# Moving the start of h, of the constant matrices and of the weight slots in SBUF: a decoder trunk on one Trainium2 core

## The chip, the core and the metric

The kernel runs on one core of a Trainium2 chip. The metric is the device time of one launch in microseconds (us). The core has a matrix engine (PE in the views; its weight loads are listed apart as PEld), a vector engine (DVE), a scalar engine (ACT), a small general engine (POOL) and a queue that only issues DMAs (SP). The operands of all of them lie in SBUF, which has 128 partitions; a tile takes the same bytes of every partition, and "address" below means the byte within a partition at which a tile begins. Matrix products go to PSUM.

## What is computed

A residual stream of 512 tokens by 1024 channels goes through two layers. Each layer has a SwiGLU block, a mixer and a second SwiGLU block, each between two RMS norms:

```python
def _swiglu(h, w_gate, w_up, w_down):
    return (jax.nn.silu(h @ w_gate) * (h @ w_up)) @ w_down

for l in range(DEPTH):                      # DEPTH = 2
    g = norm_g[l]
    f = _swiglu(_rmsnorm(x, g[0]), ffn_w_gate[l, 0], ffn_w_up[l, 0], ffn_w_down[l, 0])
    x = x + 0.5 * _rmsnorm(f, g[1])
    m = _mixer(_rmsnorm(x, g[2]), w_in[l], conv_w[l], pool_w[l], pool_scale[l], w_out[l])
    x = x + _rmsnorm(m, g[3])
    f = _swiglu(_rmsnorm(x, g[4]), ffn_w_gate[l, 1], ffn_w_up[l, 1], ffn_w_down[l, 1])
    x = x + 0.5 * _rmsnorm(f, g[5])
```

The hidden width of SwiGLU is 2816. The mixer projects `h @ w_in`, feeds the pieces to 8 heads of a stick-breaking attention, a short convolution and a pooling, and multiplies the result by `w_out`. All data are float32.

## The kernel before

**Three products for one.** Every large float32 product is made of three matmuls of a reduced float32 type: each operand is split into a high part and a low part, and the products high x high, high x low and low x high are summed in PSUM (`mm3`, L271 to L274, and `token_mms`, L384 to L393). One `mm(dst, w, r, ...)` at L222 issues each of them: `w` is the stationary operand (a load of 128 columns), `r` the moving one (up to 512 columns). Nearly all matmuls carry the line L223, so they are told apart by tile names.

**The normalised input.** `hHs` and `hLs` (L187, L188; `hh` and `hl` in the views) hold the high and low part of the normalised, transposed input h of the block at hand, 8 x 512 values to a partition each. They are allocated once and rewritten at each norm by `prenorm` (L315).

**Slots.** Everything else of size lives in 28 slots of 4 KB to a partition (`slot`, L124): raw weights as they arrive (`raw`), their high and low parts (`wh`, `wl`, made by ACT at L155 and DVE at L156), the hidden activations (`hid`), the mixer's outputs (`mix`), attention's operands (`q`, `qk`, `v`), partial sums (`f`) and gains (`g`). Smaller temporaries come from a third pool (`t`, `c`, `ss`, `pH`, `pL`).

**Which product takes what.**
- Gate and up of a SwiGLU block, and the mixer's projections (`unit`, L276): stationary a weight slot, moving h. In the views `psz<-hh,wh`, `psz<-hl,wh`, `psz<-hh,wl` (psd for the projections).
- The mixer's values (`values`, L602): stationary h, moving a weight slot: `psz<-wh,hh`, `psz<-wl,hh`, `psz<-wh,hl`.
- Down (`stream`, L395, and `by_tokens`, L421): stationary `hid`, moving a weight slot. No h in it: `psz<-wh,hid`, `psz<-wl,hid`.
- The output projection (`by_halves`, L407, and `by_tokens`): stationary `mix`, moving a weight slot. No h in it.
- Values and down have the same pattern: one block of 128 tokens of the stationary tile, then 512 columns of the moving one, three such matmuls for each pair of blocks.

**Widths.** A SwiGLU block works through its 22 blocks of hidden width in chunks of 8, 8 and 6. In the first chunk three blocks (HEAD, L32) run over half the tokens at a time, with 256 moving columns; all others have 512.

**Order.** The PE's order is written out by `line` and `after` (L214 to L220): each matmul is made to follow the one issued before it. Attention runs as a side task that is polled between matmuls, due at times counted in estimated matmul durations. Weights are loaded and split ahead as slots come free (`ahead`, L162).

**Addresses.** A pool hands out tiles in the order of the requests and rounds each tile's size up to a multiple of 32 bytes. `cpool` comes first: cst (L184), x, mat, hh, hl, ntri, none_, identr, maskr, expo (L196). Behind it follow `wpool` with the 28 slots and `apool` with the temporaries. `cst` is 50 floats (200 bytes, rounded to 224), `expo` one float (4 bytes, rounded to 32); all the others are multiples of 512 bytes.

Of the kernel before, what the change touches and what calls it, by code (L numbers as in the profile page):

```python
# [8 lines left out]
F32 = mybir.dt.float32  # L9
# [6 lines left out]
P = 128  # L16
# [42 lines left out]
C_END = C_PSC + DEPTH * 2  # L59
# [42 lines left out]
def trunk_kernel(ctx: ExitStack, tc: tile.TileContext, xt: bass.AP, wu: bass.AP,  # L102
                 consts: bass.AP, mats: bass.AP, gains: bass.AP, out: bass.AP):
    nc = tc.nc
    cpool = ctx.enter_context(tc.tile_pool(name="cpool", bufs=1))
# [75 lines left out]
        give(2 * n)  # L181


    cst = cpool.tile([P, C_END], F32, name="cst")  # L184
    x = cpool.tile([P, TBS, D], F32, name="x")
    mat = cpool.tile([P, M_END], F32, name="mat")
    hHs = cpool.tile([P, KB, T], F32R, name="hh")  # L187
# [5 lines left out]
    none_ = cpool.tile([P, P], F32R, name="none_")  # L193
    identr = cpool.tile([P, P], F32R, name="identr")
    maskr = cpool.tile([P, P], F32R, name="maskr")
    expo = cpool.tile([P, 1], F32, name="expo")  # L196
    nc.vector.memset(expo, -0.5)

    def tmp(shape=(P, T), dt=F32, tag="t", bufs=TB):
# [709 lines left out]
```

## Time and profile before

| | us |
|---|---|
| median of 3 runs | 1954.72 (1954.02 to 1956.04) |
| profiled execution, device time | 1954.8 |
| its span, first to last instruction | 1953.0 |
| PE busy | 1914.8 (98%) |
| DVE busy | 856.9 (44%) |
| ACT busy | 714.0 (37%) |

The PE has 9072 matmuls and 9072 weight loads. Its busy time is the union of the listed durations; matmuls overlap (a listed one of 512 columns lasts about 400 ns, and the next begins some 230 ns later). What a matmul costs in a stretch without waits is therefore read from the distance between starts: the length of the stretch over the count of matmuls in it. The chain of waits gives just that, since it runs from each matmul's start to the next one's.

### The profile page before, as it was taken

Reading aid. Unit: us, or ns where it says so; the run is one execution under the profiler, and the core shown is the slowest. Engines: PE = TensorE matmul, PEld = TensorE weight load, DVE = VectorE, ACT = ScalarE, POOL = GpSimd, SP = SyncE. Lnnn points to the kernel's source line nnn. Section 1 sums busy time; section 2 is a strip of 40 time slices with the busy share of each in tenths; the row PEclk is TensorE's granted clock in tenths of the full one; section 3 lists DMA queues with packets and bytes.
Section 4 is the critical chain, followed back from the end, with each engine's and each line's share of the span. In section 5 each row is a group of like instructions: output and inputs, shape, how many; then the busy total and the mean of one; then the engine's idle time right before and its main releaser. Section 6 shows DMA issues by size and latency. Waiting matters only on the chain.

```text
span 1953.0 us, 21947 instructions
## 1 busy us (share of the span) xinstructions
PE 1914.8 (98%) x9072; PEld 1588.2 (81%) x9072; DVE 856.9 (44%) x1090; ACT 714.0 (37%) x1089; POOL 40.9 (2%) x68
## 2 busy tenths in 40 slices
PE   8999999999999999999999999999999999999998
PEld 6888888878878888888898888887888888888886
DVE  4423342557766323333463232336577563223333
ACT  4323222346764323222342322224477542222221
POOL 0000000000001000000000000000000000000000
PEclk8999999999999999999999999999999999999999
DMA  5322232131122223233142322322111232322311
GB/s 211 101 83 101 85 137 79 59 116 43 44 97 109 97 68 127 76 110 106 43 152 87 109 74 80 136 81 103 66 49 44 81 141 86 106 79 85 130 65 44
DMA packets 50645, 180.17 MB, mean 92 GB/s; under 512 B 5744, under 2 KB 5872, under 8 KB 50544
## 3 DMA queue, kind: packets, MB, share of 16 engines
q1 hardware_dynamic: 50544, 178.76, 26.3%
q8 instruction: 71, 1.16, 0.2%
q14 instruction: 30, 0.25, 0.0%
HBM read 176.65 MB, written 2.10 MB: 92 GB/s over the span
## 4 chain that ended last, share of the span: by engine, by line
PE 92%; DVE 4%; ACT 2%; DMA 1%; issue 1%; POOL 0%; SPq 0%; POOLq 0%; DVEq 0%; ACTq 0%
PE psz L223 80%; PE psd L223 11%; DMA raw<-in_w_dram 1%; DVE wl L156 1%; PE psd L265 1%; ACT t L296 0%; DVE hl L331 0%; DVE pL L509 0%; DVE f L321 0%; ACT t L538 0%; ACT pH L508 0%; POOL ss L312 0%; DVE t L541 0%; DVE x L375 0%; DVE f L357 0%
## 5 line engine op out<-in xcount | busy, mean ns | idle before, releaser
L223 PE MATMUL psz<-hl,wh 128*128 128x512 f32 (+1 forms) x1536 | 574.8, 374 | 7.2 <-DVE hl L331 6.2
L223 PE MATMUL psz<-hh,wh 128*128 128x512 f32 (+1 forms) x1536 | 575.0, 374 | 1.3 <-ACT hh L330 1.3
L223 PE MATMUL psz<-hh,wl 128*128 128x512 f32 (+1 forms) x1536 | 573.9, 374 | 0.0
L156 DVE TENSOR_TENSOR wl<-raw,wh 128x1024 fp32r<-128x1024 f32 x324 | 386.5, 1209 | 322.6 <-ACT wh L155 249.9
L223 PE MATMUL psz<-wh,hid 128*128 128x512 f32 x1408 | 437.3, 390 | 0.0
L155 ACT CAST wh<-raw 128x1024 fp32r<-128x1024 f32 x324 | 328.9, 1038 | 233.9 <-PE psz L223 177.5
L223 PEld LDWEIGHTS psz<-hl,wh 128*128 128x128 f32 x1536 | 292.2, 190 | 63.3 <-DVE hl L331 7.0
L223 PEld LDWEIGHTS psz<-hh,wh 128*128 128x128 f32 x1536 | 292.0, 190 | 57.4 <-ACT hh L330 2.4
L223 PEld LDWEIGHTS psz<-hh,wl 128*128 128x128 f32 x1536 | 292.1, 190 | 55.2
L223 PEld LDWEIGHTS psz<-wh,hid 128*128 128x128 f32 x1408 | 264.3, 188 | 55.0
L223 PE MATMUL psz<-wl,hid 128*128 128x512 f32 x704 | 274.0, 389 | 0.0
L444 DVE TENSOR_TENSOR t<-t,psz 128x512 f32<-128x512 f32 x84 | 57.7, 686 | 489.0 <-PE psz L223 489.0
L445 ACT CAST hid<-t 128x512 fp32r<-128x512 f32 x88 | 54.7, 622 | 462.4 <-DVE t L444 462.4
L296 ACT ACTIVATE t<-psz 128x512 f32<-128x512 f32 (+1 forms) x136 | 77.4, 572 | 238.3 <-PE psz L223 237.5
L223 PEld LDWEIGHTS psz<-wl,hid 128*128 128x128 f32 x704 | 132.2, 188 | 27.4
L223 PE MATMUL psd<-hh,wh 128*128 128x512 f32 (+1 forms) x320 | 121.0, 378 | 0.0
L223 PE MATMUL psd<-hl,wh 128*128 128x512 f32 (+1 forms) x320 | 119.2, 373 | 0.0
L223 PE MATMUL psd<-hh,wl 128*128 128x512 f32 (+1 forms) x320 | 119.2, 373 | 0.0
L446 DVE TENSOR_TENSOR hid<-t,hid 128x512 fp32r<-128x512 f32 x88 | 60.9, 692 | 60.9 <-ACT hid L445 60.9
L223 PEld LDWEIGHTS psd<-hh,wl 128*128 128x128 f32 x320 | 60.2, 188 | 11.6
L223 PEld LDWEIGHTS psd<-hh,wh 128*128 128x128 f32 x320 | 60.2, 188 | 11.2 <-PE psd L223 0.5
L223 PEld LDWEIGHTS psd<-hl,wh 128*128 128x128 f32 x320 | 60.2, 188 | 11.2 <-issue 0.5
(99 smaller groups left out, 1377.3 us busy)
## 6 DMA issues: line engine op xcount, KB each, us to landing
raw<-in_w_dram SPq DMA_DIRECT2D x316, 512.0 KB, 3.3
g<-in_gains_dram SPq DMA_DIRECT2D x12, 512.0 KB, 5.2
x<-in_xt_dram SPq DMA_DIRECT2D x4, 512.0 KB, 8.5
raw<-in_w_dram SPq DMA_DIRECT2D x8, 256.0 KB, 2.7
out_dram<-x SPq DMA_DIRECT2D x8, 256.0 KB, 2.1
mat<-in_mats_dram SPq DMA_DIRECT2D x1, 384.0 KB, 9.4
mat<-in_mats_dram SPq DMA_DIRECT2D x1, 64.0 KB, 3.2
cst<-in_consts_dram SPq DMA_DIRECT2D x1, 25.0 KB, 9.1
```

The costliest lines, as they stand in the source:

```text
L155: nc.scalar.copy(h[:, :n], raw[:, :n])
L156: nc.vector.tensor_tensor(lo[:, :n], raw[:, :n], f32(h[:, :n]), op=ALU.subtract)
L223: ins = nc.tensor.matmul(dst, w, r, start=start, stop=stop, skip_group_check=True)
L265: ins = nc.tensor.transpose(dst, src, ident)
L296: ins = nc.scalar.activation(out_, in_, f_, **kw)
L444: nc.vector.tensor_tensor(u, g, pu, op=ALU.mult)
L445: nc.scalar.copy(t[:, 0, :], u)
L446: nc.vector.tensor_tensor(t[:, 1, :], u, f32(t[:, 0, :]), op=ALU.subtract)
```

## The change

```diff
-    cst = cpool.tile([P, C_END], F32, name="cst")
+    cst = cpool.tile([P, 64], F32, name="cst")[:, :C_END]
     x = cpool.tile([P, TBS, D], F32, name="x")
     mat = cpool.tile([P, M_END], F32, name="mat")
     hHs = cpool.tile([P, KB, T], F32R, name="hh")
...
-    expo = cpool.tile([P, 1], F32, name="expo")
+    expo = cpool.tile([P, 64], F32, name="expo")[:, 0:1]
     nc.vector.memset(expo, -0.5)
```

`cst` and `expo` are each allocated with 64 floats (256 bytes); the part in use is the same as before. What stands behind them moves. In the built programs the tiles begin here:

| tile | before | modulo 64, 256, 512 | after | modulo 64, 256, 512 |
|---|---|---|---|---|
| cst | 16512 | 0, 128, 128 | 16512 | 0, 128, 128 |
| x | 16736 | 32, 96, 352 | 16768 | 0, 128, 384 |
| mat | 33120 | 32, 96, 352 | 33152 | 0, 128, 384 |
| hh | 36704 | 32, 96, 352 | 36736 | 0, 128, 384 |
| hl | 53088 | 32, 96, 352 | 53120 | 0, 128, 384 |
| ntri, none_, identr, maskr (first) | 69472 | 32, 96, 352 | 69504 | 0, 128, 384 |
| expo | 71520 | 32, 96, 352 | 71552 | 0, 128, 384 |
| slots (first of 28) | 71552 | 0, 128, 384 | 71808 | 0, 128, 128 |
| t (first) | 186240 | 0, 128, 384 | 186496 | 0, 128, 128 |
| pH, pL (first) | 200832 | 0, 128, 128 | 201088 | 0, 128, 384 |

Slices that a matmul reads begin at multiples of 512 bytes within their tile, so the columns hold for them too. No instruction is added, removed or moved: on each of the five engines' queues the instructions, their waits and the tiles that they name stand in the same order as before, row by row; only the line numbers behind the edit are one higher.

## Rows read from the trace of the kernel before

**Rows 1.** The page: engines' busy time, then the chain's shares by line.

```profile
PE 1914.8 (98%) x9072; PEld 1588.2 (81%) x9072; DVE 856.9 (44%) x1090; ACT 714.0 (37%) x1089; POOL 40.9 (2%) x68
...
PE psz L223 80%; PE psd L223 11%; DMA raw<-in_w_dram 1%; DVE wl L156 1%; PE psd L265 1%; ACT t L296 0%; DVE hl L331 0%; DVE pL L509 0%; DVE f L321 0%; ACT t L538 0%; ACT pH L508 0%; POOL ss L312 0%; DVE t L541 0%; DVE x L375 0%; DVE f L357 0%
```

**Rows 2.** Whole chain, its long pieces: start us, length us, engine, output, matmul count.

```profile
41.08 14.20 PE psz L223 x120
58.12 322.35 PE psz L223 x1395
...
408.94 9.10 PE psz L223 x39
418.04 14.70 PE psd L223 x63
...
1540.62 20.41 PE psz L223 x90
...
1612.41 332.54 PE psz L223 x1440
```

**Rows 3.** Chain within 158:246, a stretch of gate and up; same columns.

```profile
157.89 88.20 PE psz L223 x378
```

**Rows 4.** Chain within 248:290, the stretch of down that follows.

```profile
247.95 42.17 PE psz L223 x186
```

**Rows 5.** Chain within 1022:1077, gate and up of a later block.

```profile
1022.09 55.06 PE psz L223 x236
```

**Rows 6.** Chain within 1078:1121, down of that block.

```profile
1077.85 43.31 PE psz L223 x191
```

**Rows 7.** PE groups by tiles and shape: count, busy us, mean ns, idle before.

```profile
L223 PE MATMUL psz<-hl,wh 128*128 128x512 f32 x1216 | 481.1, 396 | 0.0
...
L223 PE MATMUL psd<-hl,wh 128*128 128x512 f32 x256 | 101.2, 395 | 0.0
...
L223 PE MATMUL psz<-hh,wl 128*128 128x256 f32 x320 | 92.9, 290 | 0.0
...
L223 PE MATMUL psz<-wl,hh 128*128 128x512 f32 x64 | 25.3, 395 | 0.0
...
L223 PE MATMUL psd<-hh,wl 128*128 128x256 f32 x64 | 18.0, 281 | 0.0
```

**Rows 8.** Window of the first block: PE, PEld, DVE, ACT, POOL; clock, DMA, GB/s.

```profile
58.00:380.40 322.40, 322.40 (x1398) 262.04 (x1397) 107.95 (x115) 87.99 (x114) 1.65 (x3) 1.00 0.26 89
```

**Rows 9.** Who the PE waited for, attention: total us, times, longest.

```profile
PE psz L223 <- DVE pL L509: 5.6, 10, 1.0
...
PE psz L223 <- ACT pH L508: 3.4, 2, 2.1
```

**Rows 10.** PE timeline, attention's values, behind the output projection: start us, length.

```profile
553.16 0.39 PE L223 MATMUL psz<-pH,v 128*128 128x512 f32 x1
553.39 0.39 PE L223 MATMUL psz<-pL,v 128*128 128x512 f32 x1
553.61 0.33 PE L223 MATMUL psz<-pH,v 128*128 128x384 f32 x1
...
553.96 0.28 PE L223 MATMUL psz<-pH,v 128*128 128x256 f32 x1
554.08 0.29 PE L223 MATMUL psz<-pL,v 128*128 128x256 f32 x1
554.20 0.23 PE L223 MATMUL psz<-pH,v 128*128 128x128 f32 x1
```

**Rows 11.** PE timeline, attention's values again, behind a projection that moves h.

```profile
450.38 0.39 PE L223 MATMUL psz<-pH,v 128*128 128x512 f32 x1
450.61 0.40 PE L223 MATMUL psz<-pL,v 128*128 128x512 f32 x1
450.85 0.33 PE L223 MATMUL psz<-pH,v 128*128 128x384 f32 x1
```

## The prediction, made before the changed kernel ran

> **What bounds the kernel now.** I read the page first. PE is busy 1914.8 us of the 1953.0 us span, and the chain that ends last runs on the matmul line for 80% (psz) and 11% (psd) [rows 1]: the time is a sum of matmuls, so whatever changes the cost of one matmul shows, and hardly anything else does. Next the long pieces of the chain. The first SwiGLU block, from the end of its narrow matmuls on, is one piece of 322.35 us with 1395 matmuls and no other engine in it, and the last block one of 332.54 us with 1440 [rows 2]. In the window of the first one DVE works 107.95 us of 322.40, ACT 87.99, the DMA engines 0.26 of their time, at a granted clock of 1.00, that is 2.4 GHz [rows 8]. So in these stretches nothing feeds the PE late and the clock does not change. What is left is the matmul's own cost, and there the reader is to see that it has two values:
>
> - Gate and up: 88.20 us for 378 matmuls, 233.3 ns each [rows 3]; in a later block 55.06 us for 236, 233.3 ns [rows 5].
> - Down: 42.17 us for 186, 226.7 ns [rows 4]; in the later block 43.31 us for 191, 226.8 ns [rows 6].
>
> All have 512 moving columns, the same types and the same three-product pattern, one weight load for each matmul. The block's chain checks it: of the 1395 matmuls 912 are gate and up (38 units of 24), 483 down; 912 x 0.2333 + 483 x 0.2267 = 322.3 us, the piece's length. In the last block 912 and 528 make 332.5 us [rows 2].
>
> Which operand makes 233 of 227? The other stretches tell. The projections (moving h) take 14.70 us for 63, 233.3 ns; the mixer's values (stationary h, moving a weight slot) take 9.10 us for 39, 233.3 ns; the output projection (no h) takes 20.41 us for 90, 226.8 ns [rows 2]. Values and down differ in one thing only: the stationary tile is h in one and a slot in the other. So a matmul that reads h, on either side, costs 6.6 ns more, 2.9%. In the table of addresses h begins at 32 modulo 64, every slot at 0. The trace cannot prove that the address is the reason, but h's address is what the edit changes.
>
> **The change part by part.**
>
> Padding cst costs 56 bytes of SBUF and moves x, mat, h and the four 128x128 constants by 32 bytes. Padding expo keeps the slots at 0 modulo 64: h and slots then have the same start modulo 256, as `hid` and the weight slots of down have had all along. No instruction is added or moved, so no queue is passed and no wait arises; the DMAs, their sizes and order stay. The sum therefore has one kind of term: matmuls that read h, times 6.6 ns, as far as they lie on the chain.
>
> Gate and up with 512 columns: three groups of 1216 (one is shown) [rows 7], 3648 matmuls x 6.6 ns = 24.1 us. All lie in pieces where the chain is PE alone [rows 2], with the other engines at a third of the time [rows 8]; a PE that is 2 to 3% faster stays the bound. All of it counts.
>
> Values: three groups of 64 [rows 7], 192 x 6.6 = 1.3 us. Their longest stretch is PE alone too [rows 2]; it counts.
>
> Projections with 512 columns: three groups of 256 [rows 7], 768 x 6.6 = 5.1 us. They share the mixer with attention's chain through ACT and DVE, which does not get faster, and the PE already waits there, 5.6 us for pL and 3.4 us for pH [rows 9]. Since the PE's order is fixed, what the projections save ahead of such a wait is given back in it. Bounds: 0 and 5.1 us. I take half, 2.5 us, because most of the projections' matmuls stand ahead of such a wait or behind it with nothing to tell which.
>
> Gate, up and projections with 256 columns: three groups of 320 and three of 64 [rows 7], 1152 matmuls, now 14.20 us for 120, 118.3 ns [rows 2]. If the cost goes by columns, they fall to half of 226.7, 113.4 ns: 5.7 us gained. If what is over is fixed per matmul, they come to what attention's 256-column products with all operands at 0 modulo 64 take: 553.96 to 554.20 is 0.24 us for two, 120 ns [rows 10], 1.9 us lost. That row is the nearest, and with its steps of 10 ns it cannot be told from 118.3. I take 0 and keep both ends.
>
> Attention's constants (ntri, none_, identr as stationary, 336 short matmuls): at most 336 x 6.6 ns = 2.2 us, at least nothing; they stand beside waits, I take 0. The transposes with mat as an operand, and ACT's and DVE's work on x and h: no row shows these at another address. Three per cent either way of the transposes is under 1 us, and the engines are two thirds idle; 0.
>
> Here a rule speaks against the change. Every row above with h is dearer than every row without it [rows 3 to 6]. The Trainium skill, page "TensorE: Matmul & The Clock Gate", section "Back-to-back issue gap", gives N/2.4 + 2.5 ns between warm matmuls whatever they read, 215.8 ns for 512 columns (an estimate from that page). By it the start of a tile has no part in the time and the sum would be nothing. This trace has 226.7 and 233.3 ns at the full clock, so it does not agree; still, what it would make of the time is the first rival below.
>
> Sum: 24.1 + 1.3 + 2.5 + 0 = 27.9 us, against the profiled execution's 1954.8 us, which stands at the median of 1954.72: **1926.9 us**. The ends: 24.1 + 1.3 + 5.1 + 5.7 + 2.2 + under 1 = 39, 1916 us; 24.1 + 1.3 + 0 - 1.9 - under 1 = 23, 1932 us.
>
> **The rivals.**
>
> *The dearer matmul is h's, but not by its start.* The tiles hh and hl differ from slots in more: they are read by some 2900 matmuls of each layer, are written in four pieces by token block, and lie elsewhere in SBUF. If that is the reason, or if 32 modulo 64 is as good as 0, every matmul keeps its cost: 1954.8 us. For it: nothing in this trace has a slot at 32 modulo 64 or h at 0. Against it: the surcharge is the same to 0.1 ns with h stationary or moving, in SwiGLU blocks and mixers, and the address is what all of these share. The Trainium skill bears on it: "SBUF — State Buffer", Door 1, speaks of 16-byte lines, of which 32 modulo 64 is a whole number, and "Who interferes with whom" says that PE's two reads do not wait on anyone; by that the times would stay. No run here shows lines, and the two costs show that some operands do cost more.
>
> *A new distance.* After the change h begins at 384 modulo 512 and the slots at 128, 256 bytes apart; in down stationary and moving are 0 apart modulo 512. The trace has one pair that is 256 apart with both at 0 modulo 64: attention's values, pH and pL against v. Behind the output projection two of them take 553.16 to 553.61, 225 ns each [rows 10]; behind a projection 450.38 to 450.85, 235 ns each [rows 11]. If 235 is what that distance costs, the 4608 wide matmuls with h go from 233.3 to 235: +1.7 ns x 4608 = 7.8 us slower, 1962.6 us. It decides from 234.2 ns on (0.2% of the time over 4608 matmuls is 0.85 ns). Against it is rows 10, at the same distance; rows 11 may be what the h matmuls ahead of it leave behind.
>
> *Part of it.* One of the two reads stays dear, or attention's waits grow by more than the projections save: the gain is 4 to 20 us, 1935 to 1951 us.
>
> That the change does not do what it says is out: the addresses of the built program are those of the table.
>
> **How the numbers follow.** A measurement of this kernel can tell about 0.2%, 4 us, from no change. Forecast, 1916 to 1935 us: 0.80. More than that: 0.02. Part of it: 0.04. No change: 0.09. New distance, slower: 0.05. The predicted time is the forecast's, 1926.9 us. The range 1916 to 1935 takes in the ends of the sum and 3 us for a saving per matmul somewhat under 6.6 ns; 0.20 lies outside. Faster 0.80 + 0.02 + 0.04 = 0.86, same 0.09, slower 0.05.
>
> **What would show it.** In the changed kernel's chain the first block's long piece should be some 316.3 us (1395 x 0.2267) and a stretch of gate and up 226.7 ns per matmul, like down, which itself must not move. Values and projections the same. The narrow matmuls tell the rate from the fixed cost: 113.4 or 120 ns. If the mixers eat the projections' part, the PE's waits for pL and pH grow by about as much. The prediction is wrong if gate and up stay at 233.3 ns (first rival), rise to 235 (second), or if they fall and the blocks' pieces do not get shorter, which would mean that DVE, ACT or the DMAs had become the bound there against rows 8.

## The result and the profile after

The changed kernel takes 1926.8 us (median of 4 runs, 1925.81 to 1931.3) against 1955.13 us for the one before (median of 4): a ratio of 0.986, 95% interval 0.9848 to 0.9873, clear of no change. The forecast was 1926.9 us, range 1916 to 1935. The profiled execution took 1927.51 us, its span is 1925.7 us: 27.3 us less than before.

The long pieces of the chain answer to [rows 2]; columns: start us, length us, engine, output, count of matmuls.

```profile
41.69 14.40 PE psz L224 x120
58.97 316.23 PE psz L224 x1395
...
403.40 8.86 PE psz L224 x39
412.26 14.28 PE psd L224 x63
...
570.47 21.09 PE psz L224 x93
...
1591.22 326.44 PE psz L224 x1440
```

The first SwiGLU block's piece has the same 1395 matmuls and is 316.23 us long; it was 322.35. The last block's is 326.44, before 332.54. Values take 8.86 us for 39 (227.2 ns each, before 233.3), projections 14.28 us for 63 (226.7, before 233.3). The narrow matmuls are dearer: 14.40 us for 120 is 120.0 ns, before 118.3.

Next the chain within 158:243, gate and up as in [rows 3], and within 245:286, down as in [rows 4].

```profile
157.82 85.23 PE psz L224 x376
...
244.86 41.25 PE psz L224 x182
```

85.23 us for 376 is 226.7 ns, 41.25 us for 182 is 226.6 ns: gate and up now cost what down cost before and still costs. The window of the first block answers to [rows 8] (PE, PEld, DVE, ACT, POOL, clock, DMA share, GB/s):

```profile
58.80:375.00 316.20, 316.20 (x1397) 261.89 (x1396) 107.94 (x115) 87.84 (x113) 1.64 (x3) 1.00 0.27 91
```

DVE and ACT have the same busy time as before in a window 6 us shorter, at the same granted clock (1.00). The PE's waits in attention answer to [rows 9] (total us, times, longest):

```profile
PE psz L224 <- DVE pL L510: 6.0, 10, 1.1
...
PE psz L224 <- ACT pH L509: 2.9, 2, 1.6
```

Together 8.9 us, before 9.0: what the projections save is not given back there.

### The profile page after: what moved, and what is told of

Its sections match the earlier page's. It is cut to its first block, busy times and chain, and to the rows that moved or that the text cites. A ratio compares the mean times of both kernels' runs of the same rounds, so it can differ in the third digit from the quotient of the medians.

```text
span 1925.7 us, 21947 instructions
## 1 busy us (share of the span) xinstructions
PE 1884.1 (98%) x9072; PEld 1588.2 (82%) x9072; DVE 856.5 (44%) x1090; ACT 714.0 (37%) x1089; POOL 38.6 (2%) x68
## 4 chain that ended last, share of the span: by engine, by line
PE 92%; DVE 4%; ACT 2%; DMA 1%; issue 1%; SPq 0%; POOL 0%; DVEq 0%; POOLq 0%; ACTq 0%
PE psz L224 80%; PE psd L224 10%; DMA raw<-in_w_dram 1%; DVE wl L156 1%; PE psd L266 1%; ACT t L297 1%; DVE pL L510 0%; DVE t L542 0%; ACT t L539 0%; ACT pH L509 0%; DVE hl L332 0%; DVE f L358 0%; DVE pH L507 0%; ACT wh L155 0%; DVE f L322 0%
## 5 line engine op out<-in xcount | busy, mean ns | idle before, releaser
L224 PE MATMUL psz<-hl,wh 128*128 128x512 f32 (+1 forms) x1536 | 566.9, 369 | 6.3 <-DVE hl L332 5.4
L224 PE MATMUL psz<-hh,wh 128*128 128x512 f32 (+1 forms) x1536 | 567.2, 369 | 4.1 <-ACT hh L331 4.1
L224 PE MATMUL psz<-hh,wl 128*128 128x512 f32 (+1 forms) x1536 | 566.2, 369 | 0.0
L155 ACT CAST wh<-raw 128x1024 fp32r<-128x1024 f32 x324 | 328.7, 1039 | 233.0 <-PE psz L224 178.3
L297 ACT ACTIVATE t<-psz 128x512 f32<-128x512 f32 (+1 forms) x136 | 77.5, 572 | 227.2 <-PE psz L224 226.3
L224 PEld LDWEIGHTS psz<-wl,hid 128*128 128x128 f32 x704 | 132.2, 188 | 27.3
```

The lines of the kernel that those rows point to most:

```text
L155: nc.scalar.copy(h[:, :n], raw[:, :n])
L224: ins = nc.tensor.matmul(dst, w, r, start=start, stop=stop, skip_group_check=True)
L297: ins = nc.scalar.activation(out_, in_, f_, **kw)
```

## The experiments

The time came out as forecast, but the trace of before could not say why a matmul that reads h was dear. There h stood at 32 modulo 64 and, with that, 32 bytes away from the slots modulo 256: at 96, the slots at 128. Two theories, as the expectations name them:

- **A, the start.** A matmul is dear when an operand begins at 32 modulo 64. The prediction leaned on this one.
- **B, the distance.** It is cheap when the stationary and the moving operand begin at the same place modulo 256. Where each of them begins does not matter.

In the changed kernel both conditions hold. Four kernels set them apart by moving tiles. "Distance" below is the moving operand's start less the stationary one's, in bytes modulo 256; in the kernel before it was 224 for gate, up and projections (96 less 128) and 32 for the values. Each was timed beside the kernel before on one chip (1955.08 us, 16 runs).

**e1: h at 0 modulo 64, but 64 bytes away from the slots.**

```diff
-    cst = cpool.tile([P, 64], F32, name="cst")[:, :C_END]
+    cst = cpool.tile([P, 80], F32, name="cst")[:, :C_END]
...
-    expo = cpool.tile([P, 64], F32, name="expo")[:, 0:1]
+    expo = cpool.tile([P, 48], F32, name="expo")[:, 0:1]
```

> Edit to the changed kernel: cst gets 80 floats and expo 48, so that x, mat, h and the constants begin at 192 modulo 256 (0 modulo 64) while the slots stay at 128 modulo 256. Theory A, the start: a matmul is dear when an operand begins at 32 modulo 64, whatever the distance to the other: gate, up, projections and values stay at 226.7 ns per wide matmul, down at 226.7, the time stays at 1925 to 1929 us. Theory B, the distance: it is cheap only where both operands have the same start modulo 256: gate and up go back to about 233.3 ns, down stays at 226.7, the time goes back to about 1953 to 1957 us.

1936.0 us (1934.04 to 1936.43, 4 runs), ratio 0.9902 (0.9886 to 0.9919). Some of its chain's long pieces:

```profile
58.21 318.43 PE psz L224 x1395
...
405.16 9.11 PE psz L224 x39
414.27 14.70 PE psd L224 x63
430.57 8.93 PE psd L224 x39
...
1369.23 14.44 PE psd L224 x63
```

Neither theory's number. The block's piece is 318.43 us; 483 of its matmuls are down, at 226.7 ns 109.5 us, which leaves 208.9 us for 912 of gate and up, 229.1 ns. The values, at the opposite distance (192), take 9.11 us for 39, 233.6 ns. A falls, since all starts are at 0 modulo 64; B has the right sign, but 64 is a cheaper distance than 224 or 32. And one thing more: the 63 projections take 14.70 us (233.3 ns) in the first mixer, 14.44 us (229.2 ns) in the second, though the operands are of the same kind and the values ahead of them cost 233 ns in both.

**e2: only cst padded; h at 0 modulo 64, slots and temporaries at 32.**

```diff
-    expo = cpool.tile([P, 64], F32, name="expo")[:, 0:1]
+    expo = cpool.tile([P, 1], F32, name="expo")
```

> Only the padding of cst: expo is one float again, so h begins at 128 modulo 256 (0 modulo 64) and the slots and temporaries at 160 (32 modulo 64). Theory A: every wide matmul has at least one operand at 32 modulo 64: gate and up 233.3 ns, down and the output projection 233.3 too (2496 matmuls more than in the kernel before, 16 us), 1968 to 1975 us; more if two such operands cost twice (down at 240). Theory B: gate and up 233.3 (32 bytes apart), down 226.7 (0 apart), 1953 to 1957 us.

1953.85 us (10 runs), ratio 0.9999 (0.999 to 1.0008): half of the edit alone gives nothing. Its chain, first the first block's piece and the values, then within 248:289, down:

```profile
57.62 322.33 PE psz L224 x1395
...
408.99 9.10 PE psz L224 x39
...
247.90 41.25 PE psz L224 x182
```

The pieces are those of the kernel before to 0.02 us [rows 2]. Down has both operands at 32 modulo 64 now and still takes 226.6 ns. Theory A wanted some 16 us more than the kernel before here.

**e3: only expo padded; everything at 32 modulo 64, h and slots 0 apart.**

```diff
-    cst = cpool.tile([P, 64], F32, name="cst")[:, :C_END]
+    cst = cpool.tile([P, C_END], F32, name="cst")
```

> Only the padding of expo: h, slots and temporaries all begin at 96 modulo 256 (32 modulo 64), the same start for both operands everywhere. Theory A: all wide matmuls 233.3 ns, 1968 to 1975 us, or more if two such operands cost twice. Theory B: all at 226.7 ns, 1925 to 1929 us.

1926.48 us (1925.29 to 1928.3, 4 runs), ratio 0.9857 (0.9842 to 0.9872), the changed kernel's time. Its chain, the last row within 245:286 (down):

```profile
58.65 316.23 PE psz L224 x1395
...
403.09 8.85 PE psz L224 x39
...
245.00 41.03 PE psz L224 x181
```

The same pieces as in the changed kernel, with no tile of weight or of h at a multiple of 64. This settles it between the two: the 28 us of the change come from h and slots having the same start modulo 256, and the multiples of 64 have no part in them. The padding of expo alone would have done.

**e4: hh 0 apart from the slots, hl 32 bytes.**

```diff
+    cpool.tile([P, 8], F32, name="gap1")
     hLs = cpool.tile([P, KB, T], F32R, name="hl")
+    cpool.tile([P, 8], F32, name="gap2")
...
-    expo = cpool.tile([P, 64], F32, name="expo")[:, 0:1]
+    expo = cpool.tile([P, 48], F32, name="expo")[:, 0:1]
```

> In the changed kernel 32 bytes of padding between hh and hl, and 32 behind hl, with expo at 48 floats: hh at 128 modulo 256, hl at 160 (32 modulo 64), slots at 128. One of the three products reads hl. Theory A, each matmul pays for its own moving operand: hl,wh 233.3 ns, the other two 226.7, a mean of 228.9 in gate and up, and about 10 us of the 28 are lost, 1934 to 1939 us. If the cost sat in a state that the stretch keeps and not in the single matmul, all three would be at 233.3 and the time near 1953.

1948.96 us (1947.06 to 1950.9, 7 runs), ratio 0.9969 (0.9958 to 0.998). Chain within 159:246, gate and up, and three matmuls of the PE's timeline there (start us, length):

```profile
158.83 87.34 PE psz L226 x377
...
181.37 0.39 PE L226 MATMUL psz<-hh,wl 128*128 128x512 f32 x1
181.60 0.40 PE L226 MATMUL psz<-hh,wh 128*128 128x512 f32 x1
181.84 0.39 PE L226 MATMUL psz<-hl,wh 128*128 128x512 f32 x1
```

231.7 ns on the mean, where a third of the matmuls at 233.3 and the rest at 226.7 would be 228.9; the expectation's other branch, all three at 233.3 and some 1953 us, does not come out whole either. The products that read hh, 0 apart, are dear too: over 160:245 the next start in the trace comes 230.2 ns after `hh,wl`, 231.7 after `hh,wh` and 233.0 after `hl,wh`. So one matmul in three at distance 32 makes its neighbours dear as well: the cost is not each matmul's own.

**m1: distances by themselves.** No trunk, two tiles, 72 matmuls for each distance; DVE, ACT and the DMA queues have nothing to do meanwhile (from the second series on).

```diff
+    for c, (n, so, mo, reps) in enumerate(CASES):
+        for i in range(reps):
+            mm(pp[c % 2][:, :n], sta[:, so + (i % 8) * P:so + (i % 8) * P + P], mov[:, mo + 512 * (i % 2) * (n == 512):][:, :n])
```

> Not the trunk: after 24 warming matmuls it runs series of 72 matmuls, each with its own weight load, from two tiles alone, and hands x through as its output. Series by distance, that is the moving start minus the stationary start in bytes: with 512 columns 0, 32, 64, 96, 128, 160, 192, 224, then 16, 48, 80, 112, 144, 240, 4, 8; with 256 and with 128 columns 0, 32, 64, 128, 192, 224; last three series with both tiles' starts shifted by 32 bytes (distances 0, 64, 32). Every engine but the PE is idle. Theory A (start modulo 64): 226.7 ns at 0, 64, 128, 192 and 233.3 at the rest, and 233.3 in all of the last three. Theory B (distance modulo 256, the kinds of the trunk's runs): 226.7 at 0, 233 at 32 and 224, 229 to 233 at 64 and 192, and the last three as at 0, 64, 32; at the distances never seen (96 to 160) it says nothing, 220 to 240. If it is neither, but what else runs (ACT, DVE, DMA writing SBUF), all series are equal here.

The PE's timeline has one row for each series (start us, length); the cost of a matmul is the distance to the next row's start over 72. The first three rows are 512 columns at distance 32, 64 and 96. Then 256 columns at 0 (275.69), 32, and at 192 (309.84) and 224. Last 512 columns with both tiles' starts shifted by 32 bytes, at 0, 64 and 32.

```profile
24.50 16.97 PE L119 MATMUL odd<-mov,sta 128*128 128x512 f32 x72
41.30 16.65 PE L119 MATMUL even<-mov,sta 128*128 128x512 f32 x72
57.79 16.97 PE L119 MATMUL odd<-mov,sta 128*128 128x512 f32 x72
...
275.69 8.80 PE L119 MATMUL even<-mov,sta 128*128 128x256 f32 x72
284.32 8.65 PE L119 MATMUL odd<-mov,sta 128*128 128x256 f32 x72
...
309.84 8.35 PE L119 MATMUL even<-mov,sta 128*128 128x256 f32 x72
318.02 8.68 PE L119 MATMUL odd<-mov,sta 128*128 128x256 f32 x72
...
374.73 16.56 PE L119 MATMUL even<-mov,sta 128*128 128x512 f32 x72
391.12 16.66 PE L119 MATMUL odd<-mov,sta 128*128 128x512 f32 x72
407.62 16.94 PE L119 MATMUL even<-mov,sta 128*128 128x512 f32 x72
```

16.80 us for 72 is 233.3 ns at distance 32, 16.49 is 229.0 at 64. With both starts shifted by 32 bytes, distance 0 takes 16.39 us (227.6 ns, the first few at the change of series included) and 64 takes 16.50 (229.2), where theory A wanted 233.3 for both. The trunk's numbers return with nothing running but the PE: no other engine and no DMA is needed for the surcharge. All distances, worked out the same way (ns for one matmul):

```
512 columns   32: 233.3   64: 229.0   96: 233.5  128: 233.3  160: 234.3  192: 233.3  224: 233.3
              16: 231.7   48: 230.0   80: 231.0  112: 231.1  144: 233.2  240: 233.3    4: 236.7    8: 231.7
256 columns    0: 119.9   32: 117.9   64: 117.9  128: 118.6  192: 113.6  224: 118.3
```

The unshifted series at 0, the first behind the warming matmuls, has 229.7 ns with that change included and 226.7 from the ninth matmul on. With 512 columns none of the others is cheaper than that. With 256 columns 0 is the dearest and 192 the cheapest. With 128 columns all distances take 111 to 112 ns.

**m2: which pair, and which period.**

```diff
+            s, m = so[i % 2] // 4 + (i % 8) * P, mo[i % 2] // 4
+            mm(pp[c % 2][:, :n], sta[:, s:s + P], mov[:, m:m + n])
```

> Series of 72 matmuls from two tiles again, no trunk. First, with 512 columns: distance 0; stationary and moving starts alternating together between 0 and 32 bytes (each matmul's own operands 0 apart, but while it streams the next one's weights are loaded from 32 bytes beside it); distance 0; then alternating crosswise (own operands 32 apart, but the weights loaded during each stream 0 apart from it). If the pair that counts is a matmul's own two operands: 226.7 and 233.3 ns. If it is the stream and the weight load that runs beside it: 233.3 and 226.7. Then distances 0, 256, 512, 768, 1024, 288, 448: if only the distance modulo 256 counts, 226.7 for the first five, 233.3 for 288 (as 32) and 448 (as 192); 176, 208, 248, 252 fill the gaps, 229 to 237. With 256 columns 0, 256, 192, 448: 120, 120, 113.4, 113.4 by the same rule; 16 to 240 between 113 and 122. With 384 columns 0, 32, 64, 128, 192, 224: 173.3 and around 175.

PE's timeline: alternating together (25.24), 0, alternating crosswise (58.27), 0, 256, 512, then further on 288 (156.47), 448 and 176; last 256 columns at 256 (265.29), 192 and 448.

```profile
25.24 16.86 PE L124 MATMUL odd<-mov,sta 128*128 128x512 f32 x72
41.94 16.50 PE L124 MATMUL even<-mov,sta 128*128 128x512 f32 x72
58.27 16.75 PE L124 MATMUL odd<-mov,sta 128*128 128x512 f32 x72
74.86 16.49 PE L124 MATMUL even<-mov,sta 128*128 128x512 f32 x72
91.19 16.48 PE L124 MATMUL odd<-mov,sta 128*128 128x512 f32 x72
107.51 16.48 PE L124 MATMUL even<-mov,sta 128*128 128x512 f32 x72
...
156.47 16.97 PE L124 MATMUL odd<-mov,sta 128*128 128x512 f32 x72
173.27 16.96 PE L124 MATMUL even<-mov,sta 128*128 128x512 f32 x72
190.07 16.95 PE L124 MATMUL odd<-mov,sta 128*128 128x512 f32 x72
...
265.29 8.80 PE L124 MATMUL even<-mov,sta 128*128 128x256 f32 x72
273.93 8.34 PE L124 MATMUL odd<-mov,sta 128*128 128x256 f32 x72
282.11 8.32 PE L124 MATMUL even<-mov,sta 128*128 128x256 f32 x72
```

The period is settled for the distances tried: 91.19 to 107.51, 16.32 us for 72, is 226.7 ns at 256, and 512, 768 and 1024 are the same; 288 costs what 32 costs (16.80 us, 233.3 ns) and 448 what 192 costs (233.3 ns; with 256 columns 113.3 ns at 448 and 113.6 at 192). Of the distances that fill the gaps, 176 takes 233.2 ns, 208 234.7 and 248 230.0; 252, four bytes short of 256, takes only 227.1, under the expected 229, while 4 took 236.7 in m1. With 384 columns 0 takes 173.3 ns, the others 173.3 to 176.8. Which pair counts is not settled: alternating together gives 16.70 us, 231.9 ns, crosswise 16.59 us, 230.4 ns, and each theory wanted one of them at 226.7. It is left open.

**k1, k2, k4: narrow matmuls at another distance.** Since 256 columns were cheapest at 192 in m1, the narrow matmuls' weights were placed 64 bytes into their slot. That takes wider slots, and to make room one slot and one side buffer less:

```diff
-SLOTS = 28
+SLOTS = 27
+SHIFT = 16
...
-CB = 5
+CB = 4
...
-        return wpool.tile([P, 2, T], dt, tag="w", bufs=SLOTS, name=name)
+        t = wpool.tile([P, 2 * T + 64], dt, tag="w", bufs=SLOTS, name=name)
+        return t[:, at:at + 2 * T].rearrange("p (a b) -> p a b", a=2)
...
+        at = SHIFT if UNITS[i][0] in ("gate", "up") and UNITS[i][3] < HEAD else 0
...
```

`at` goes to the two slots that hold a unit's split weights. k2 is the control with SHIFT = 0, k4 has SHIFT = 36 (144 bytes, distance 112).

> The changed kernel with slots of 4352 bytes (27 instead of 28, and 4 instead of 5 buffers of side tiles, to fit); the split weights of the narrow matmuls begin 64 bytes into their slot, so that h is 192 modulo 256 from them; everything else stays 0 apart. If the distance sets the narrow matmul's cost as in the two-tile series, the narrow ones take 113.4 ns instead of 120.4, at most 8 us over 1152; since part of them stands beside waits for h, 3 to 7 us less than the control that follows. If the distance does not carry over, the same as the control.

> Control for the last: the same 27 wider slots and 4 side buffers, with the narrow matmuls' weights at the start of their slot (0 apart). Narrow ones 120.4 ns; 1926 to 1930 us if the lost slot and side buffer cost nothing, more if they do.

k1: 1922.86 us (1920.82 to 1925.6, 5 runs); k2: 1927.47 us (1924.55 to 1928.61, 4 runs). 4.6 us between the medians, within what was expected. Then, on one chip, the changed kernel, k4 and k1 again:

> The changed kernel itself, timed on the same chip as the two that follow, so that they can be set against it: 1925 to 1929 us, 226.7 ns for wide matmuls with h, 120 ns for narrow ones.

> As the kernel with the narrow weights 64 bytes into wider slots, but 144 bytes in, so that h is 112 modulo 256 from them, the other distance at which the two-tile series took 113.3 ns with 256 columns. If the distance alone sets the cost, 113.3 ns in all four SwiGLU blocks and 2 to 5 us less than the 64-byte version, whose narrow matmuls took 113.3 ns in the first block and 117.8 in the other three. If what ran just before also counts, again some blocks at a second value (117 to 120), and 1919 to 1927 us.

> The 64-byte version again beside the changed kernel on one chip: 3 to 5 us less than it (narrow matmuls at 113.3 ns in the first block and 117.8 in the others against 120); no difference beyond 2 us if the earlier 1922.9 against 1926.8 was the chip.

The changed kernel 1925.67 us (1925.17 to 1929.46, 4 runs); k4 1927.34 us (1926.41 to 1928.94); k1 again 1923.34 us (1920.97 to 1924.53, 5 runs). k1's five runs all lie below the changed kernel's four; 2.3 us, 0.12%, between the medians is little, and less than the 3 to 5 us expected. k4 gains nothing, outside both branches of its expectation. The chains' narrow pieces of k1's second run, in the order of the blocks:

```profile
40.62 13.60 PE psz L227 x120
...
621.10 14.13 PE psz L227 x120
...
990.70 14.13 PE psz L227 x120
...
1570.08 14.13 PE psz L227 x120
```

and the first of k4:

```profile
41.62 14.40 PE psz L227 x120
```

k1's narrow matmuls take 113.3 ns in the first block and 117.8 in the other three, for the same distances; k4's take 120.0 in all four, where the two-tile series took 114 at that distance. So the distance alone does not set the cost. m2 shows it within one series, 256 columns at 112; its chain within 315.9:317.2 and within 317.3:324:

```profile
315.99 1.30 PE even L124 x11
...
317.30 6.81 PE even L124 x60
```

The first matmuls take 118 ns, the last sixty 113.5, from the same two tiles and with the PE alone at work. That a stretch keeps a pattern of reads it came in with would fit this, e4 and k1, but no run here shows such a pattern. Where all matmuls of a trunk's long stretch were 0 apart the value hardly varied at the full clock: 226.6 to 227.9 ns for down, gate and up, projections and values, 120.0 for narrow ones.

**k3: fewer narrow matmuls.**

```diff
-HEAD = 3
+HEAD = 2
```

> The changed kernel with HEAD = 2: one pair of blocks less of narrow matmuls in each SwiGLU block. Two narrow ones cost 240.8 ns, a wide one 226.7, so 192 pairs fewer save 2.7 us if no new wait for h arises; if the shorter head no longer covers the norm of the second half of the tokens, PE's waits for hh and hl grow and it is the same or slower, 1926 to 1932 us.

1930.89 us (1929.28 to 1931.68, 4 runs), some 4 us slower than the changed kernel instead of 2.7 faster. Of the PE's waits (total us, times, longest) those for h:

```profile
PE psz L224 <- DVE hl L332: 7.0, 6, 3.1
...
PE psz L224 <- ACT hh L331: 4.0, 5, 2.6
```

11.0 us in 11 waits; the changed kernel has 9.5 us in 4 (5.4 for hl, 4.1 for hh). That is 1.5 us of the 7 missing, from one execution of each, and the same waits were 7.5 us in the kernel before; where the rest went was not followed up.

## Why the prediction was right, and where it was not

**The bound and the term that carries it: right.** Gate and up were to fall to 226.7 ns and the first block's piece to 316.3 us; they are 226.7 ns and 316.23 us. The four blocks' long pieces lost 6.12, 6.10, 6.11 and 6.10 us (322.35, 322.33, 322.34 and 332.54 before), together 24.4 us against the 24.1 of the sum. The assumption that nothing else becomes the bound held: DVE, ACT and DMA do the same work in the shorter window.

**Mixers: right in kind, the half was a little low.** The sum counted 1.3 us for the values and 2.5 of the projections' 5.1. From the start of the values to that of the last part of the output projection the chain of before runs 399.68 to 578.74 and 1364.03 to 1540.62, that of after 394.34 to 570.47 and 1344.72 to 1519.05: 2.9 and 2.3 us less, 5.2 us against 3.8. The waits did not grow (8.9 us against 9.0). Some of the first mixer's gain is the clock's. The output projection's first 48 matmuls took 12.59 us there before, at a mean granted clock of 0.87, and 10.96 after, at 1.00: 1.6 us. In the stretch ahead of them it is the other way round: 42.05 us before from 524.10 to 566.15, 42.71 after from 516.80 to 559.51, where the granted clock was 0.95 from 527 on, while the second mixer, at 1.00 in both, became 0.3 us shorter there. That takes back about 1 us, which leaves some 2.3 us for each mixer, 4.5 in all (an estimate from these stretches). What attention's 336 short matmuls, put at 0, have in it was not separated.

**Narrow matmuls: put at 0, they lost 1.9 us.** The sum took 0 between -5.7 and +1.9 us. 120.0 less 118.3 ns is 1.7 ns, over 1152 matmuls 1.9 us lost: the end at which the surplus is fixed per matmul, and just the 120 ns read off attention's products in [rows 10]. The nearest row had the answer and was set aside for the coarseness of its digits. (The 192 of them that the prediction calls projections belong to gate and up as well; the sum is the same.)

**The total: in part luck.** 24.4 + 5.2 - 1.9 = 27.7 us against 27.3 measured; the remaining 0.4 us lies between the long pieces, around the norms, where the chain became 2.3 us longer, 1.9 of it by the narrow matmuls. That the time meets the forecast to 0.1 us is luck: the mixers gained 1.4 us more than the sum has and the narrow matmuls lost 1.9 that it put at 0, and the four runs spread over 5.5 us.

**The reason: wrong where it named one.** The prediction read the two costs rightly as one of h's address, and tied them to "32 modulo 64, every slot at 0" as its working idea; it also noted that h and slots would have the same start modulo 256, as `hid` and the weights of down always had, but did not weigh the one against the other. e3 keeps every tile at 32 modulo 64 and has the whole gain, e1 has every tile at 0 modulo 64 and two thirds of it, e2 swaps the sides and has none. It is the distance. The trace of before held the two together and could not have told them apart; the edit satisfied both, so the number came out all the same, and that was luck. With the padding of expo alone, e3's layout, the same reasoning would have forecast 2496 x 6.6 ns = 16.5 us more than before, 1971 us, and missed by 45.

**The rivals.** "Not by its start" falls with e2 against e3: tiles of the same use and order, other distances, other times. One clause of it holds, though: 32 modulo 64 is as good as 0 (e3). "A new distance" was the right kind of question with the wrong period: 256 bytes apart costs what 0 costs (m2). Its one piece of evidence, 235 ns in [rows 11], is answered by the same place in the changed kernel, where attention's operands are 256 apart as before and the projections ahead of them have become cheap:

```profile
443.84 0.39 PE L224 MATMUL psz<-pH,v 128*128 128x512 f32 x1
444.06 0.39 PE L224 MATMUL psz<-pL,v 128*128 128x512 f32 x1
444.29 0.33 PE L224 MATMUL psz<-pH,v 128*128 128x384 f32 x1
```

The two wide ones take 0.45 us now, 225 ns each, and 0.46 (230) in e1, where those projections cost 229. So it was that rival's last clause, what the h matmuls ahead leave behind. It does not explain everything: e1's first projections cost 233.3 ns in one mixer and 229.2 in the other behind the same values.

**The rule set aside.** The Trainium skill's N/2.4 + 2.5 ns ("TensorE: Matmul & The Clock Gate", "Back-to-back issue gap") is given there for a matmul by itself, not for a stream of weight loads and matmuls in pairs. It holds for no series here, which all load weights for each float32 matmul: the cheapest with 512 columns, in m2 with everything else idle at a mean granted clock of 1.0, is 226.7 ns against its 215.8.

## What to carry to other kernels

Where one weight load goes with each wide matmul of this float32 type, look at the start of both operands modulo 256 and give the tiles of both the same one: an odd-sized constant ahead of them in a pool is enough to spoil it, 2.9% of each matmul here, and no busy share, wait or clock shows it. It is seen by dividing stretches without waits by their count of matmuls and comparing kinds that have the same shape. Before the finding is turned into a rule (a multiple of 64, a special distance for narrow matmuls), move the tiles so that the candidates come apart: two builds that differ in padding did that here.

## What the runs showed of the hardware

- In series with the PE alone at work (m1, m2), the cost of a matmul of 512 columns goes by the distance between the starts of the stationary and the moving float32 operand: 226.7 ns at 0, 256, 512, 768 and 1024 bytes, 229.0 at 64, 233.3 at 32, 128, 192 and 224, 236.7 at 4.
- At distance 0, 256, 384 and 512 columns take 120.0, 173.3 and 226.7 ns: 53.3 ns for each 128 columns, and 13.3 ns more for each matmul (m2).
- With 256 columns the order of the distances is another: 120 ns at 0, 113.3 to 113.6 at 192; with 128 columns, 111 to 112 ns at all distances.
- The distance alone does not set the cost of a stretch. What ran just before counts: attention's wide values took, at one and the same place, 235, 230 and 225 ns behind projections at 233.3, 229 and 226.7 (before, e1, after), and one matmul in three at distance 32 brought the mean of all three to 231.7 in e4. The same kind of matmuls at the same distance also had two costs where no cause was found: 233.3 and 229.2 ns in the two mixers of e1, 113.3 and 117.8 in k1. How this state is made was not found, nor which weight load counts, the matmul's own or the one beside its stream.
